# Second mixer: two modulation vectors to TensorE's column groups, GpSimd's low parts of weights to VectorE

## The chip, the cores and the metric

The kernel is one program on one core of a Trainium2 chip. The metric is the device time of the program in microseconds; of the kernel before there are three runs, 2885.76, 2887.93 and 2890.27 us, median 2887.93.

## The reference

Two transformer blocks run one after the other on 256 tokens of width 2048, in float32, batch 1. Each block makes six modulation vectors from a conditioning vector, mixes tokens, and runs a feed-forward part:

```python
mod = silu(c) @ ada_w + ada_b                # 2048 x 12288: six vectors of 2048
sh1, sc1, g1, sh2, sc2, g2 = split(mod, 6)   # numbers 0 to 5
u = rms_norm(h, norm_mix_g) * (1 + sc1) + sh1
h = h + g1 * hybrid_mixer(u, ...)            # u @ w_in, attention of four kinds, @ w_out
u = rms_norm(h, norm_ffn_g) * (1 + sc2) + sh2
h = h + g2 * swiglu(u, ...)
```

The first block has a mixer of two recurrent kinds and a squared-ReLU feed-forward part; the second block, shown above, has a mixer with four kinds of attention (in the code fox, nsa, dil and diff) and ends with one more norm. The change touches the second block's vector 4 (the scale sc2, needed for the feed-forward input) and vector 2 (the gate g1, needed at the mixer's end), and the weights of that mixer.

## The kernel before, in words

All matrices come from HBM once, in pieces ("items") of 128 partitions x 1024 float32, 512 KB, each into one of five buffers named raw (RAW_BUFS, line 26). There are two kinds of items, in one list that is fixed ahead (lines 1908 to 1945): weights of a product, and pieces of a modulation matrix that are strewn between them.

Products run in two float32r parts. For a weight item, ScalarE writes the high part wh from raw, and an engine that is chosen per item writes the low part wl = raw - wh (`prep`, line 274). TensorE then does three matmuls for each weight tile: high x high, high x low and low x high. Four buffers hold pairs of wh and wl. Which engine makes wl is decided by `l_eng` (line 350) from the mark `low` that line 1939 puts on an item: 0 is VectorE; 1 and 2 lead to GpSimd for all or for every second item; 3 compares the two engines' times in a cost model kept in the code (class `_Clock`) and takes GpSimd if it would be done at most 3 us after VectorE. The table LOW (lines 1901 to 1903) sets 3 for the second mixer's input products (qG, kvH, sv, qA, kB, qC, kD, dv0, dv1, qE, kF, fdv) and 2 for most of its output product (pA, 0 to 3). A few places in the code of a stage's turn call `prep(pool)` and fix GpSimd for one item.

A modulation vector comes from 32 items. In one way (`cg` false), VectorE does two accumulating steps for each item, acc = raw x c + acc, on 128 x 512 elements, with one value of the conditioning per partition; the partitions are summed later. In the other way (`cg` true, `ada_cg`, line 320), two items are held until both are there, and TensorE does four matmuls with the conditioning as stationary operand, 32 columns wide, each in its own quarter of TensorE's columns; after four pairs the sum is taken from PSUM by ScalarE (a column vector) or VectorE (a row vector). The first block's vectors 0, 1, 3, 4 and 2 go the second way before; all others go the first way. Two items are then placed in the list at once (line 1942).

The order of every engine's instructions is fixed when the program is built. The builder emits the big matmuls in order, and after each weight tile the function `fill` (line 439) emits other work: steps of evacuations, attention steps (generators), and the next `prep`, by the same cost model. Every instruction emitted updates the model, so a change of one engine's work moves the places of others.

In the trace all engine instructions have the line 169 of a recording helper, so they are told apart by their tiles: raw, wh, wl as above; hTh, hTl and o2h, o2l, oq2h, oq2l the high and low parts of activations; g a PSUM tile of a big product; mx a PSUM tile of small products (three buffers); S score tiles in SBUF; acc sums of modulation vectors; ada the PSUM tile of the second way; csil the conditioning.

Of the kernel before, what the change touches and what calls it, by code (L numbers as in the profile page):

```python
# [178 lines left out]
def two_blocks(ctx, tc, I, out):  # L179
# [47 lines left out]
    items = []  # L227
# [5 lines left out]
    def add_w(pieces, nk, n):  # L233
        items.append({"pieces": pieces, "nk": nk, "n": n})
        return len(items) - 1

    def add_ada(blk, v, q, kp, fin, row, cg):
        items.append({"ada": (blk, v, q, kp), "fin": fin, "row": row, "cg": cg})
# [457 lines left out]
    def col_gen(blk, v, q):  # L696
        a = accs.pop((blk, v, q))
        name = (("mix1", "ffn1"), ("mix2", "ffn2"))[blk][v // 3]
        p = mx()
        if blk == 0:  # L700
            for k in range(4):
                mm(p[:, k:k + 1], a[:, k * 128:(k + 1) * 128], ones[:, 0:1])
        else:
            for k in range(4):
                pe.transpose(p[:, k * 128:(k + 1) * 128], a[:, k * 128:(k + 1) * 128], ident)
            red = small([4], "red")
            junk = wt("junk")
            for k in range(4):
                act.activation(junk[:, k * 128:(k + 1) * 128], p[:, k * 128:(k + 1) * 128], AF.Copy, accum_out=red[:, k:k + 1])
            p = red  # L710
            yield
        b0 = 128 + blk * 64 + (v // 3) * 32 + (v % 3) * 16 + q * 4
        ks = slice(q * 4, q * 4 + 4)
        if v % 3 == 0:
            dve.tensor_add(AB[name][1][:, ks], p[:, 0:4], cols[:, b0:b0 + 4])
        else:
            tmp = small([4], "colt")
            dve.tensor_add(tmp, p[:, 0:4], cols[:, b0:b0 + 4])
            dve.scalar_tensor_tensor(AB[name][0][:, ks], tmp, 1.0, NORM[name][:, ks], op0=ADD, op1=MUL)

    def row_gen(blk, v, q, key, mul):
        while key not in gws:
            yield
        while not slots:
            yield
        slot = k, p = slots.popleft()
        a = accs.pop((blk, v, q))
        t = p.tile([128, UK * 512], FR, name="ah", tag=f"wh{k}")
        h, l = t[:, 0:512], t[:, 512:1024]
        act.activation(h, a, AF.Copy)  # L730
        dve.tensor_tensor(l, a, h, op=SUB)
        yield 3
        if slot[0] < st["n"]:
            slots.append(slot)
        p = mx()
        mm(p, ones_r, h, True, False)
        mm(p, ones_r, l, False, True)
        o = gws[key][:, q * 512:(q + 1) * 512]
        if mul:
            dve.tensor_tensor(o, p, o, op=MUL)  # L740
        else:
            act.activation(o, p, AF.Copy)
        gwn[key] = gwn.get(key, 0) + 1
# [4 lines left out]
    def ada_vecs(blk, vs, key=None, mul=False, cg=False):  # L748
        n = 8 * len(vs)
        for q in range(4):  # L750
            for kp in range(n):
                fin = None
                if kp == n - 1:
                    if key is None:
                        fin = lambda q=q: urgent.extend((clk.wr[clk.key(accs[blk, v, q])][0] + 0.2, col_gen(blk, v, q)) for v in vs)
                    else:
                        fin = lambda q=q: urgent.append((clk.wr[clk.key(accs[blk, vs[0], q])][0] + 0.2, row_gen(blk, vs[0], q, key, mul)))
                ADA.append((blk, vs, q, kp, fin, key is not None, cg))
# [1127 lines left out]
    ada_vecs(1, (0, 1))  # L1886
    ada_vecs(1, (3,))
    n_b = len(ADA)
    ada_vecs(1, (4,))
    ada_vecs(1, (2,), "g1")  # L1890
    n_c = len(ADA)
    ada_vecs(1, (5,), "g2")

    def weight(k):
        if k[0] in ("oB", "pB") or k == "fv" or k[1:] == (0, 0) and k[0] in ("f1", "ga") or k in (("f1", 0, 1), ("f2", 3, 2), ("f2", 3, 3)):
            return 0.0
        if k in ("qG", "kvH", "sv"):
            return 0.5
        return 1.0

    LOW = {k: 1 for k in ("qG", "kvH", "sv", "qA", "kB", "qC", "kD", "dv0", "dv1", "qE", "kF", "fdv")}
    LOW.update({k: 3 for k in LOW if isinstance(k, str)})
    LOW.update({("pA", c): 2 for c in range(4)})
    ai = n_first
    wide = [blocks[n, 0] for n in ("hq", "hf", "hv", "hg", "zq", "zk", "zv", "gg")]
    q_items = [ADA[q * 16:q * 16 + 16] for q in range(4)]
# [21 lines left out]
    for endkey, ntot in phases:  # L1928
        hi = order.index(endkey) + 1
        tot = sum(len(blocks[k].us) * weight(k) for k in order[lo:hi])  # L1930
        tot = tot * 0.5 if endkey[0] == "up" else tot - (3 if endkey[0] == "pA" else 0 if endkey == "fdv" else 24)
        a0, na = ai, ntot - ai
        done = 0.0
        for k in order[lo:hi]:
            b = blocks[k]
            b.idx = []
            for u in b.us:
                b.idx.append(add_w(*u))
                items[-1]["low"] = k in LOW and (LOW[k] if LOW[k] == 3 else len(b.idx) % LOW[k] == 0)
                done += weight(k)  # L1940
                while ai < ntot and (ai - a0) < na * done / tot:
                    for _ in range(1 + ADA[ai][6]):
                        add_ada(*ADA[ai])
                        ai += 1
        lo = hi
# [200 lines left out]
    b = blocks["f2", 3, 3]  # L2146
# [90 lines left out]
    b = blocks["pB", 0]  # L2237
# [63 lines left out]
    b = blocks["dn", 2, 3]  # L2301
# [45 lines left out]
```

## Time and profile before

| | |
|---|---|
| runs, median | 2887.93 us (2885.76 to 2890.27) |
| profiled execution | 2885.77 us, span 2883.8 us, mean granted TensorE clock 0.972 |
| TensorE matmul (PE) | 2713.4 us busy, 94% |
| VectorE (DVE) | 1783.3 us busy, 62% |
| ScalarE (ACT) | 1246.2 us busy, 43% |
| GpSimd (POOL) | 464.1 us busy, 16% |
| moved | 643.93 MB, mean 223 GB/s |

A busy time counts from an instruction's start to its end, so an instruction that is held up while it runs counts as busy for longer. PE durations overlap, since matmuls are pipelined: how long one really takes of the engine is the distance between two starts. A wait is listed by what ended it. The second mixer lies between some 1632 and 2080 us from the span's start.

### The profile page before, as it was taken

Reading aid. Unit: us, or ns where it says so; the run is one execution under the profiler, and the core shown is the slowest. Engines: PE = TensorE matmul, PEld = TensorE weight load, DVE = VectorE, ACT = ScalarE, POOL = GpSimd, SP = SyncE. Lnnn points to the kernel's source line nnn. Section 1 sums busy time; section 2 is a strip of 40 time slices with the busy share of each in tenths; the row PEclk is TensorE's granted clock in tenths of the full one; section 3 lists DMA queues with packets and bytes.
Section 4 is the critical chain, followed back from the end, with each engine's and each line's share of the span. In section 5 each row is a group of like instructions: output and inputs, shape, how many; then the busy total and the mean of one; then the engine's idle time right before and its main releaser. Section 6 shows DMA issues by size and latency. Waiting matters only on the chain.

```text
span 2883.8 us, 44820 instructions
## 1 busy us (share of the span) xinstructions
PE 2713.4 (94%) x17761; PEld 2377.2 (82%) x17761; DVE 1783.3 (62%) x2228; ACT 1246.2 (43%) x1963; POOL 464.1 (16%) x306
## 2 busy tenths in 40 slices
PE   6988999999979999999998899998979999999998
PEld 3666788877869899897997798886769989998997
DVE  1443563655568877778765657677866665554456
ACT  3322354344554444444444436454454443443443
POOL 1000123123040000000002465554520000000001
PEclk8998999999989999999999899999989999999999
DMA  9876775684548888988865675667747777656654
GB/s 337 241 210 194 206 254 181 209 270 147 167 142 295 310 292 296 317 279 296 296 211 168 180 216 166 199 207 239 252 144 233 232 237 236 187 184 193 183 183 146
DMA packets 346594, 643.93 MB, mean 223 GB/s; under 512 B 31488, under 2 KB 50640, under 8 KB 344976
## 3 DMA queue, kind: packets, MB, share of 16 engines
q1 hardware_dynamic: 343296, 628.26, 68.0%
q10 hardware_dynamic: 2336, 10.42, 0.9%
q8 instruction: 139, 2.28, 0.3%
q0 software_dynamic: 752, 2.39, 0.2%
q14 instruction: 71, 0.58, 0.1%
HBM read 636.27 MB, written 4.19 MB: 222 GB/s over the span
## 4 chain that ended last, share of the span: by engine, by line
PE 52%; DVE 7%; DMA 5%; issue 3%; ACT 3%; POOL 2%; SPq 0%; ACTq 0%; POOLq 0%; DVEq 0%
PE g L169 50%; DMA raw<-in_w_ff_dram 3%; PE mx L169 3%; DVE acc L169 2%; DVE wl L169 2%; ACT wh L169 1%; DMA raw<-in_ada_w_dram 1%; POOL wl L169 1%; DVE xres L169 1%; POOL y L169 1%; DMA raw<-in_w_in_dram 0%; DVE S L169 0%; ACT sq L169 0%; DVE y L169 0%; ACT hTh L169 0%
## 5 line engine op out<-in xcount | busy, mean ns | idle before, releaser
L169 DVE TENSOR_TENSOR wl<-raw,wh 128x1024 fp32r<-128x1024 f32 x696 | 871.8, 1258 | 720.6 <-ACT wh L169 713.3
L169 ACT ACTIVATE wh<-raw 128x1024 fp32r<-128x1024 f32 (+2 forms) x817 | 846.5, 1044 | 1078.8 <-PE g L169 683.3
L169 PE MATMUL g<-hTh,wh 128*128 128x256 f32 x3328 | 959.0, 288 | 4.0 <-ACT wh L169 2.3
L169 PE MATMUL g<-hTh,wl 128*128 128x256 f32 x3328 | 945.2, 284 | 1.9 <-POOL wl L169 1.2
L169 PE MATMUL g<-hTl,wh 128*128 128x256 f32 x3328 | 944.0, 284 | 0.3 <-DVE hTl L169 0.3
L169 PEld LDWEIGHTS g<-hTh,wh 128*128 128x128 f32 x3328 | 637.8, 192 | 42.9 <-issue 36.0
L169 PEld LDWEIGHTS g<-hTl,wh 128*128 128x128 f32 x3328 | 640.0, 192 | 1.9 <-DVE hTl L169 0.6
L169 PEld LDWEIGHTS g<-hTh,wl 128*128 128x128 f32 x3328 | 637.4, 192 | 3.0 <-POOL wl L169 1.7
L169 DVE SCALAR_TENSOR_TENSOR acc<-raw,csil,acc 128x512 f32<-128x512 f32 x432 | 391.9, 919 | 64.3 <-DMA raw<-in_ada_w_dram 57.7
L169 PE MATMUL g<-wh,rh 128*128 128x512 f32 x864 | 339.7, 393 | 0.0
L169 PE MATMUL g<-wh,rl 128*128 128x512 f32 x864 | 339.2, 393 | 0.0
L169 PE MATMUL g<-wl,rh 128*128 128x512 f32 x864 | 339.0, 392 | 0.0
L169 POOL TENSOR_TENSOR wl<-raw,wh 128x1024 fp32r<-128x1024 f32 (+3 forms) x121 | 275.8, 2288 | 236.4 <-ACT wh L169 232.3
L169 POOL TENSOR_TENSOR y<-y,gw 128x512 f32<-128x512 f32 x22 | 32.1, 1474 | 1308.1 <-ACT sq L169 749.9
L169 PEld LDWEIGHTS g<-wh,rl 128*128 128x128 f32 x864 | 162.6, 188 | 36.2
L169 PEld LDWEIGHTS g<-wl,rh 128*128 128x128 f32 x864 | 162.7, 188 | 35.7
L169 PEld LDWEIGHTS g<-wh,rh 128*128 128x128 f32 x864 | 162.6, 188 | 35.5
L169 PE MATMUL g<-wh,hTh 128*128 128x512 f32 (+3 forms) x344 | 136.5, 397 | 12.2 <-ACT hTh L169 12.2
L169 PE MATMUL g<-wl,hTh 128*128 128x512 f32 (+3 forms) x344 | 128.4, 373 | 2.5 <-POOL wl L169 2.5
L169 PE MATMUL g<-wh,hTl 128*128 128x512 f32 (+3 forms) x344 | 128.9, 375 | 0.1
L169 PE MATMUL ada<-raw,csil 128*32 128x512 f32 x640 | 107.7, 645 | 16.5 <-DMA raw<-in_w_ada_dram 14.7
L169 PEld LDWEIGHTS g<-wh,hTh 128*128 128x128 f32 x344 | 67.8, 197 | 35.9 <-ACT hTh L169 14.9
(460 smaller groups left out, 2762.5 us busy)
## 6 DMA issues: line engine op xcount, KB each, us to landing
raw<-in_w_ff_dram SPq DMA_DIRECT2D x256, 512.0 KB, 5.3
raw<-in_w_ada_dram SPq DMA_DIRECT2D x192, 512.0 KB, 5.0
raw<-in_ada_w_dram SPq DMA_DIRECT2D x192, 512.0 KB, 5.0
raw<-in_w_in_dram SPq DMA_DIRECT2D x176, 512.0 KB, 5.8
raw<-in_ffn_w_gate_dram SPq DMA_DIRECT2D x88, 512.0 KB, 4.0
raw<-in_ffn_w_up_dram SPq DMA_DIRECT2D x88, 512.0 KB, 3.7
raw<-in_ffn_w_down_dram SPq DMA_DIRECT2D x88, 512.0 KB, 4.1
raw<-in_w_out_dram SPq DMA_DIRECT2D x60, 512.0 KB, 4.6
```

Source lines behind the costliest of these rows:

```text
L169: r = f(out, *a, **kw)
```

## The change

Vectors 4 and 2 of the second block are made in the second way. The table LOW goes, and every item's mark becomes 0, so that VectorE makes all low parts except those that `prep(pool)` fixes.

```diff
     n_b = len(ADA)
-    ada_vecs(1, (4,))
-    ada_vecs(1, (2,), "g1")
+    ada_vecs(1, (4,), cg=True)
+    ada_vecs(1, (2,), "g1", cg=True)
     n_c = len(ADA)
...
-    LOW = {k: 1 for k in ("qG", "kvH", "sv", "qA", "kB", "qC", "kD", "dv0", "dv1", "qE", "kF", "fdv")}
-    LOW.update({k: 3 for k in LOW if isinstance(k, str)})
-    LOW.update({("pA", c): 2 for c in range(4)})
...
-                items[-1]["low"] = k in LOW and (LOW[k] if LOW[k] == 3 else len(b.idx) % LOW[k] == 0)
+                items[-1]["low"] = 0
```

On TensorE, in the product qG of the second mixer (a difference; + is what the change adds):

```order
 L169 MATMUL g<-hTl_13933,wh 128x256
 L169 MATMUL g<-hTh_13929,wl 128x256
+L169 MATMUL ada<-raw,csil 32x512 x4
 L169 MATMUL g<-hTh_13929,wh 128x256
 L169 MATMUL g<-hTl_13933,wh 128x256
```

Groups of four such matmuls stand at 32 more places, between the big matmuls; nothing else is added to TensorE.

On VectorE, ahead of the score tiles of the dil attention (S, with their row maxima dl), before:

```order
L169 TENSOR_TENSOR o2l_14435<-mx,o2h_14434 64x256
L169 SCALAR_TENSOR_TENSOR acc<-raw,csil,acc 128x512 x14
L169 TENSOR_TENSOR colt<-red,cols 128x4
L169 SCALAR_TENSOR_TENSOR Affn_128<-colt,cols 128x4
L169 SCALAR_TENSOR_TENSOR acc<-raw,csil,acc 128x512 x4
L169 SCALAR_TENSOR_TENSOR S_17271<-cb,mx 128x384 x3
L169 TENSOR_REDUCE dl_17272<-S_17271 128x3 x2
```

and in the changed kernel:

```order
L169 TENSOR_TENSOR wl<-raw,wh 128x576
L169 TENSOR_TENSOR colt<-red,cols 128x4
L169 SCALAR_TENSOR_TENSOR Affn_128<-colt,cols 128x4
L169 TENSOR_TENSOR o2l_14441<-mx,o2h_14440 128x256
L169 TENSOR_TENSOR wl<-raw,wh 128x576 x3
L169 TENSOR_TENSOR wl<-raw,wh 128x1024 x4
L169 SCALAR_TENSOR_TENSOR S_17284<-cb,mx 128x384 x3
L169 TENSOR_REDUCE dl_17285<-S_17284 128x3 x2
```

The accumulating steps are gone from VectorE's queue, and low parts that GpSimd made stand there instead.

On GpSimd, at the start of the second mixer (a difference; S and lfp are tiles that it clears, kvH a projection that it copies):

```order
-L169 TENSOR_TENSOR wl<-raw,wh 128x1024 x10
-L169 TENSOR_TENSOR wl<-raw,wh 128x560 x4
-L169 COPY S_14440<-kvH 64x256
-L169 COPY S_14440<-kvH 64x255
-L169 COPY S_14443<-kvH 64x256
-L169 COPY S_14443<-kvH 64x255
-L169 TENSOR_TENSOR wl<-raw,wh 128x560 x4
-L169 TENSOR_TENSOR wl<-raw,wh 128x1024 x32
-L169 TENSOR_TENSOR wl<-raw,wh 128x576 x12
```

Of these the four copies come again in the changed kernel, and none of the low parts. The five `prep(pool)` items of the turn at the mixer's end stay on GpSimd.

## Rows read from the trace of the kernel before

**Rows 1.** The page: span, GpSimd's busy share and TensorE's granted clock in 40 slices

```profile
span 2883.8 us, 44820 instructions
...
POOL 1000123123040000000002465554520000000001
PEclk8998999999989999999999899999989999999999
```

**Rows 2.** Busy time by stage (from:to, length, engines with instruction counts, clock, DMA)

```profile
core 0: us, PE busy (x) PEld busy (x) DVE busy (x) ACT busy (x) POOL busy (x), PEclk, DMA share, GB/s
300.00:700.00 400.00, 390.91 (x2780) 317.37 (x2781) 232.53 (x389) 164.13 (x330) 97.25 (x78) 1.00 0.69 221
1632.00:2080.00 448.00, 412.46 (x2819) 368.63 (x2819) 316.30 (x425) 218.21 (x481) 239.48 (x120) 0.95 0.67 213
2150.00:2800.00 650.00, 650.00 (x4713) 617.26 (x4712) 362.98 (x357) 270.60 (x287) 3.53 (x2) 1.00 0.67 208
1632.00:1640.00 8.00, 5.14 (x23) 4.83 (x23) 6.70 (x13) 5.50 (x8) 2.58 (x1) 0.64 0.95 266
1700.00:1720.00 20.00, 20.00 (x176) 19.66 (x176) 13.04 (x17) 6.26 (x10) 11.65 (x5) 0.74 0.70 212
```

**Rows 3.** TensorE's waits, 1632 to 2080 (total us, times, longest)

```profile
PE mx L169 <- DVE S L169: 16.0, 12, 4.3
...
PE g L169 <- POOL wl L169: 2.7, 4, 1.2
...
PE g L169 <- ACT wh L169: 2.3, 1, 2.3
```

**Rows 4.** VectorE's groups, 1632 to 2080 (busy us, mean ns, idle before)

```profile
L169 DVE SCALAR_TENSOR_TENSOR acc<-raw,csil,acc 128x512 f32<-128x512 f32 x127 | 166.9, 1314 | 54.8 <-DMA raw<-in_ada_w_dram 52.2
L169 DVE TENSOR_TENSOR wl<-raw,wh 128x1024 fp32r<-128x1024 f32 x21 | 35.3, 1679 | 13.6 <-ACT wh L169 11.8 <-PE mx L169 1.8
```

**Rows 5.** The same on VectorE, 2200 to 2500 and 2200 to 2800 (min/median/max ns)

```profile
L169 DVE SCALAR_TENSOR_TENSOR acc<-raw,csil,acc x48: 742/748/754, 2202.7 to 2446.5; 128x512 f32<-128x512 f32 x48
...
L169 DVE TENSOR_TENSOR wl<-raw,wh x212: 1214/1225/1586, 2200.4 to 2797.8; 128x1024 fp32r<-128x1024 f32 x106
```

**Rows 6.** GpSimd's low parts, 1632 to 2080, by shape

```profile
L169 POOL TENSOR_TENSOR wl<-raw,wh 128x1024 fp32r<-128x1024 f32 x76 | 187.1, 2470 | 186.7 <-ACT wh L169 183.4 <-PE mx L169 2.2 <-PE g L169 0.9
L169 POOL TENSOR_TENSOR wl<-raw,wh 128x576 fp32r<-128x576 f32 x16 | 25.2, 1581 | 15.2 <-ACT wh L169 14.6 <-DMA raw<-in_w_in_dram 0.6
L169 POOL TENSOR_TENSOR wl<-raw,wh 128x560 fp32r<-128x560 f32 x8 | 11.9, 1492 | 4.6 <-ACT wh L169 4.4
```

**Rows 7.** Timeline near 1880: VectorE, GpSimd, TensorE (start us, us, [idle before])

```profile
1874.98 11.19 DVE L169 SCALAR_TENSOR_TENSOR acc<-raw,csil,acc 128x512 f32<-128x512 f32 x4 [1.30 <-DMA raw<-in_ada_w_dram]
...
1877.56 5.31 POOL L169 TENSOR_TENSOR wl<-raw,wh 128x1024 fp32r<-128x1024 f32 x2 [0.27 <-ACT wh L169]
...
1886.69 0.54 PE L169 MATMUL mx<-kD,qC 64*128 64x128 f32 x1 [4.32 <-DVE S L169]
```

**Rows 8.** Timeline of TensorE in the first mixer, around one column group

```profile
425.59 0.28 PE L169 MATMUL g<-hTl,wh 128*128 128x256 f32 x1
425.71 0.28 PE L169 MATMUL g<-hTh,wl 128*128 128x256 f32 x1
425.92 1.06 PE L169 MATMUL ada<-raw,csil 128*32 128x512 f32 x8
426.92 0.39 PE L169 MATMUL g<-hTh,wh 128*128 128x256 f32 x1
427.14 0.28 PE L169 MATMUL g<-hTl,wh 128*128 128x256 f32 x1
```

**Rows 9.** Waits of the SP queue and of VectorE, 1632 to 2080

```profile
SPq L169 <- POOL wl L169: 219.2, 85, 9.5
...
DVE acc L169 <- DMA raw<-in_ada_w_dram: 54.2, 19, 14.1
```

**Rows 10.** Column groups, 300 to 700: busy by engine; TensorE's idle before them

```profile
300.00:700.00 400.00, 56.63 (x344) 8.69 (x344) 2.71 (x4) 4.17 (x7) 1.00 0.69 221
...
  DMA raw<-in_w_ada_dram: 7.3, 5
```

## Prediction

> **What bounds the kernel now.** I read the page first. TensorE is busy nearly all of the span; GpSimd has one long busy stretch, slices 25 to 28 of 40, and in the same slices the granted clock dips [rows 1]. That stretch is the second mixer, and it is where the diff acts. Next I cut the program into stages [rows 2]. In the feed-forward stage from 2150 to 2800 TensorE is busy 650.00 of 650.00 us at full clock, with every low part made on VectorE and GpSimd next to idle. In the second mixer, 1632 to 2080, it is busy 412.46 of 448.00 us at a mean granted clock of 0.95. So TensorE is the bound in both; the mixer alone has slack, of two kinds. It idles 448.00 - 412.46 = 35.5 us. And the clock has two levels, so a mean of 0.95 means that 448 x 0.05 = 22.4 us of full-speed work is lost to the lower one. A change here can give back at most 35.5 + 22.4 = 57.9 us.
>
> What does TensorE wait for there? The table of waits [rows 3] has eleven lines: the largest is the score tiles S on VectorE, 16.0 us in 12 waits; low parts from GpSimd end only 2.7 us directly; 2.3 us belong to ScalarE. So VectorE is late, though busy only 316.30 of 448.00 us [rows 2]. Why shows in its own groups. One accumulating step of a modulation vector costs 1314 ns on the mean here, 127 times, and a low part 1679 ns [rows 4]; the same instructions cost 748 ns (742 to 754) and 1225 ns after 2200, where GpSimd does nothing [rows 5]. The difference is GpSimd's subtractions, 76 of 2470 ns, 16 of 1581 and 8 of 1492 [rows 6]. The timeline shows one case [rows 7]: from 1874.98 four accumulating steps last 11.19 us instead of 4 x 0.75 = 3.0, under GpSimd's low parts, and TensorE waits 4.32 us for the score tile queued behind them.
>
> That the two engines exclude each other is what the Trainium skill says too (SBUF — State Buffer, section SBUF: two separate sides): a VectorE instruction with two SBUF inputs and a GpSimd instruction that reads SBUF take one shared port pair in turn, for the whole instruction. The stretched steps agree [rows 4, 5]; by that rule the change frees VectorE wholly, which is the first rival below.
>
> **VectorE and GpSimd, part by part.** The two vectors are 64 items of two steps, 128 steps; 127 begin in this window and go: -166.9 us of VectorE time [rows 4]. The 100 low parts of GpSimd come: 76 x 1.225 = 93.1 us [rows 5]; the 24 narrow ones have no undisturbed row on VectorE, so I scale by GpSimd's ratio, 1.225 x 1581/2470 = 0.78, 18.8 us. The 21 low parts already on VectorE fall from 1679 to 1225 ns, -9.5 us. VectorE ends near 316.3 - 166.9 + 93.1 + 18.8 - 9.5 = 252 us, 56% of the stage: it does not become the bound. GpSimd loses 187.1 + 25.2 + 11.9 = 224 us, none of it on TensorE's path except those 2.7 us. GpSimd keeps the five low parts that the code of the turn at 2080 asks of it by name; I cost that at nothing, since the order of instructions has them where they were. Eight evacuations of the new sums (one on ScalarE or VectorE for each vector quarter) are hidden behind TensorE's stream.
>
> **TensorE pays.** Every pair of items becomes one group of four matmuls, 32 groups. Their price stands in the first mixer, where other vectors already go this way [rows 8]: the matmul before starts at 425.71, 0.12 behind its predecessor, and its successor would come at 425.83; the group starts at 425.92, the next at 426.92 and the one after it only at 427.14, 0.22 behind instead of 0.12. So a group pushes the stream back by 427.14 - 0.12 - 425.83 = 1.19 us, not the 1.06 of its own row. 32 x 1.19 = 38.1 us, all of it on the engine that bounds. Nothing hides it except slack that it fills.
>
> The Trainium skill has a rule against the change here (TensorEngine Tiling (Array Packing), section Tiling Modes, Key Properties): changing the tiling mode drains the engine. The 0.09 us ahead of the group and the 0.10 behind agree; without such a cost the sum would be 32 x 1.00 = 32.0.
>
> **What TensorE gets back.** Of the 35.5 us of idle, 8.00 - 5.14 = 2.9 lie ahead of 1640 [rows 2], most of it ScalarE's 2.3 [rows 3], and stay. Of the other 32.6 I let 6 stay: the score matmuls write three PSUM buffers that VectorE must empty, and it still works 56% of the time, so the 12 waits for S keep about 0.5 us each. That is -26.6 us. Of the 22.4 us of clock, 8 x 0.36 = 2.9 fall before 1640 and 20 x 0.26 = 5.2 between 1700 and 1720, where TensorE is busy 20.00 of 20.00 us with narrow matmuls [rows 2]: these stay. The other 14.3 follow waits and go in their proportion, 26.6/32.6: -11.7 us. Gain 38.3 us, bounded by 0 and by 32.6 + 14.3 = 46.9.
>
> **A wait is added.** A group stands in TensorE's queue and needs both weight items landed; behind it stand all the mixer's matmuls. Before, VectorE took this wait: 54.2 us in 19 waits [rows 9]. In the first mixer, 43 groups in 400 us take 56.63 us of TensorE against 43 x 1.06 = 45.6, so 11.0 us are waits inside groups, and 7.3 us more are shown as waits for the transfer [rows 10]: 0.43 a group. With 32 groups in 448 us, a third less dense, I scale it to 32 x 0.43 x (32/448)/(43/400) = 9 us. The bounds: 0, since the SP queue now waits 219.2 us for GpSimd to free raw buffers [rows 9] and VectorE will free them sooner; and half of VectorE's 54.2, 27 us, since one wait can serve two items. I take 9, by the nearest row.
>
> **Sum.** 38.1 + 9 - 38.3 = +8.8 us. The profiled execution took 2885.77 us for its span of 2883.8, so 2894.6; it stands 2.2 us below the median 2887.93, which carries the sum to 2896.7. I take 2896. Its own range, from waits left at 3 to 12 us and transfers at 5 to 13: 2889 to 2905.
>
> **Rivals.**
> First, faster: the port was the whole trouble. All 32.6 us of waits and the 14.3 us of clock go, and transfers land in time because raw buffers come free sooner: 38.1 - 46.9 = -8.8 us, 2879. For it speak the stretched steps [rows 7] and the stage after 2150 with no idle at all [rows 2]; against it that the scores' three buffers remain, and that the first mixer, with other GpSimd work but the same groups, still idles 400.00 - 390.91 = 9.1 us. It decides where transfers and the waits that are left stay together under 46.9 - 38.1 - 5.8 = 3 us, the 5.8 being what a measurement can tell (below).
>
> Second, slower: the transfers' wait moves to TensorE in full. At 27 us the sum is 38.1 + 27 - 38.3 = +27, 2915. It takes the forecast's place from some 15 us of such waits on. For it: VectorE's wait is real and long, and 64 of these items pass through five raw buffers together with the weights. Against it: the first mixer's 0.43 a group at a DMA share of 0.69, where this stage has 0.67 [rows 2].
>
> Third, a wash: waits go as forecast and transfers cost little, 38.1 + 2 - 40 = 0, 2888.
>
> Fourth, low parts late: 100 of them now stand in VectorE's queue, each behind ScalarE's high part, and the score tiles behind them; if that keeps every wait, 38.1 + 9 = +47, 2935.
>
> **How the numbers follow.** Below 0.2% (5.8 us) a measurement of this kernel cannot tell a difference from none. Forecast 0.48, of it 0.36 slower and 0.12 same; first rival 0.24, of it 0.20 faster and 0.04 same; second 0.12, slower; third 0.12, of it 0.02 faster and 0.10 same; fourth 0.04, slower. That makes faster 0.22, same 0.26, slower 0.52. The range runs from the first rival's 2879 to the second's 2915: half of the first and of the second, and the fourth, lie outside.
>
> **What the profile after would show.** Right: VectorE's low parts at 1.23 us throughout the mixer and its busy time near 250 us; 32 more groups of 1.0 us on TensorE; TensorE's waits for S and for the other VectorE tiles under 10 us; the granted clock of the stage near 0.98; the stage some 9 us longer. Wrong: the stage shorter than 448 us (the gain was under-counted), waits of TensorE for the modulation weights above 15 us (second rival), or waits for low parts or S as long as now (fourth).

## Result, and the profile after

The changed kernel is slower by half a per cent: 2907.55 us median (2902.08 to 2911.49, 8 runs) against 2891.49 (2883.72 to 2900.01, 8 runs) for the kernel before, a ratio of 1.0053 [1.0035, 1.0070]. In the terms of the prediction's sum that is 2887.93 x 0.0053 = 15.3 us, where +8.8 was forecast. The two profiled executions, 2905.57 and 2885.77 us, lie 19.8 us apart, 4 us more than the medians; the one of the kernel before was at the quick end of its runs. The sums below are of these two executions.

The page after, in the rows that answer to [rows 1]: the span, GpSimd's busy tenths and TensorE's granted clock in 40 slices.

```profile
span 2903.7 us, 45170 instructions
...
POOL 1000123122030000000002000000230000000001
PEclk8998999999989999999999998999989999999999
```

GpSimd's long stretch, slices 23 to 29 before [rows 1], is gone, as the change says. In this part of the span the clock dipped in slices 23 and 30 before, at the two ends of the stage; now it dips in 25 and 30, so one dip has moved from the stage's start into its middle.

To compare like with like I cut the stage at the same two pieces of work in both kernels, from the evacuation of the first mixer's last projection to GpSimd's first addition to the residual stream. For the kernel before, the stage by windows (from:to, length, busy time and instructions of PE, PEld, DVE, ACT, POOL, clock, DMA share, GB/s), and then the stretch 1725 to 1790:

```profile
1631.20:2078.80 447.60, 412.06 (x2820) 368.24 (x2820) 315.42 (x426) 218.02 (x482) 238.28 (x120) 0.95 0.67 212
...
1725.00:1790.00 65.00, 61.25 (x499) 56.27 (x498) 54.53 (x90) 40.74 (x118) 32.45 (x14) 1.00 0.57 179
```

The same for the changed kernel:

```profile
1627.30:2098.60 471.30, 446.21 (x3081) 368.25 (x3080) 235.54 (x404) 222.16 (x486) 15.15 (x20) 0.97 0.63 202
...
1725.00:1790.00 65.00, 53.61 (x403) 46.48 (x402) 32.12 (x69) 35.99 (x99) 0.53 (x1) 0.87 0.45 137
```

The stage grew by 471.3 - 447.6 = 23.7 us, and the other stages gave back 4. TensorE's idle time fell from 447.60 - 412.06 = 35.5 us to 471.30 - 446.21 = 25.1, and the full-speed work lost to the lower clock, by the mean, from 22.4 us to 471.3 x 0.03 = 14.1. But take the 65 us from 1725 on. There TensorE idled 3.75 us at full clock before; now it idles 11.4 us, at a mean clock of 0.87, which is another 65 x 0.13 = 8.5 us (a part of it falls into the idle time itself and costs nothing, see the last section). Nearly half of all idle time that the stage has now, and more than half of its lost clock, lie in this one stretch, which was among the best before.

What TensorE waits for in the changed kernel, 1628 to 2098 (total us, times, longest), answers to [rows 3]:

```profile
PE mx L169 <- DVE S L169: 11.6, 4, 6.0
PE ada L169 <- DMA raw<-in_ada_w_dram: 4.8, 9, 1.5
PE g L169 <- ACT wh L169: 3.5, 3, 1.6
PE g L169 <- DVE wl L169: 2.4, 5, 0.8
PE mx L169 <- DVE lfp L169: 2.0, 1, 2.0
...
```

The score tiles S are the largest line still, but its shape is another: 12 waits became 4, and two of these are nearly all of the 11.6 us. TensorE's timeline shows them (start us, us, [idle before, and what ended it]):

```profile
1753.50 0.58 PE L169 MATMUL mx<-ksw,qG 64*128 64x128 f32 x1 [6.05 <-DVE S L169]
...
1766.38 0.58 PE L169 MATMUL mx<-kvH,qG 64*128 64x128 f32 x1 [4.91 <-DVE S L169]
```

Both lie in the stretch 1725 to 1790. Why was VectorE late with S there, when it was busy only 32.12 of 65 us? Its timeline around the first of them:

```profile
1744.19 1.81 DVE L169 TENSOR_REDUCE ns<-S 128x4 f32<-128x512 f32 x2
1750.25 1.23 DVE L169 TENSOR_TENSOR wl<-raw,wh 128x1024 fp32r<-128x1024 f32 x1 [4.24 <-ACT wh L169]
...
1751.76 1.23 DVE L169 TENSOR_TENSOR wl<-raw,wh 128x1024 fp32r<-128x1024 f32 x1
1752.90 1.01 DVE L169 SCALAR_TENSOR_TENSOR S<-cb,mx 128x384 f32<-128x384 f32 x2
```

and ScalarE's in the same microseconds, first and last of eight exponentials, and the high parts behind them:

```profile
1744.91 0.40 ACT L169 ACTIVATE S<-S,ns 128x128 f32<-128x128 f32 x1 [2.83 <-DVE ns L169]
...
1748.68 0.49 ACT L169 ACTIVATE S<-S,ns 128x256 f32<-128x256 f32 x1
...
1749.18 1.99 ACT L169 ACTIVATE wh<-raw 128x1024 fp32r<-128x1024 f32 x2
```

Read it from the end. TensorE waits until 1753.50 for a PSUM buffer. VectorE empties it into S from 1752.90 on, not because it was busy, but because two low parts stand ahead of S in its queue, and the first of them waited 4.24 us, until 1750.25, for ScalarE's high part. ScalarE made that high part only from 1749.18 on, since eight softmax exponentials stood ahead of it. A low part that has nothing to do with the scores joins the two queues, and what was parallel becomes a chain: exponentials, high part, low part, next scores.

The same place in the kernel before. GpSimd, then ScalarE, then VectorE:

```profile
1747.88 2.38 POOL L169 TENSOR_TENSOR wl<-raw,wh 128x1024 fp32r<-128x1024 f32 x1 [7.03 <-ACT wh L169]
```

```profile
1746.76 1.04 ACT L169 ACTIVATE wh<-raw 128x1024 fp32r<-128x1024 f32 x1
```

```profile
1744.95 1.01 DVE L169 SCALAR_TENSOR_TENSOR S<-cb,mx 128x384 f32<-128x384 f32 x2
...
1750.48 1.02 DVE L169 SCALAR_TENSOR_TENSOR S<-cb,mx 128x384 f32<-128x384 f32 x2
```

ScalarE's high part stood behind the exponentials there too. But it was GpSimd that stood still for it, 7.03 us, with nothing of TensorE's behind it, while VectorE went on to S. In sum, VectorE's waits for high parts in the changed kernel, 1628 to 2098, are

```profile
DVE wl L169 <- ACT wh L169: 159.9, 83, 6.6
```

GpSimd had 183.4 + 14.6 + 4.4 = 202 us of such waits before [rows 6], and VectorE 11.8 at its large low parts [rows 4]; so some three quarters of GpSimd's waits now stand in VectorE's queue. Two of the 83, of 4.24 and 6.62 us, stand ahead of the two long waits for S.

The price of a group and the waits for transfers, on TensorE's timeline of the changed kernel:

```profile
1657.31 0.28 PE L169 MATMUL g<-hTh,wl 128*128 128x256 f32 x1
1657.52 1.06 PE L169 MATMUL ada<-raw,csil 128*32 128x512 f32 x8
1658.52 0.39 PE L169 MATMUL g<-hTh,wh 128*128 128x256 f32 x1
1658.74 0.28 PE L169 MATMUL g<-hTl,wh 128*128 128x256 f32 x1
...
1689.23 1.05 PE L169 MATMUL ada<-raw,csil 128*32 128x512 f32 x4 [1.46 <-DMA raw<-in_ada_w_dram]
1690.54 1.05 PE L169 MATMUL ada<-raw,csil 128*32 128x512 f32 x4 [0.25 <-DMA raw<-in_ada_w_dram]
```

The undisturbed group costs 1658.74 - 1657.31 - 2 x 0.12 = 1.19 us, as forecast. The other one came in two halves: the first item's two matmuls ran, and the second item was not there yet. Its halves take 1.05 us each, as long as the whole. So a late second item costs more than its listed wait. Five groups are split like this, with starts 1.31, 1.75, 1.35, 1.28 and 1.84 us apart. Three more of the 31 in this stage ran in two halves too, though no wait is listed for them: they show as one row of about twice the length, 2.16, 2.15 and 2.02 us instead of 1.06. The first of them:

```profile
1784.25 2.16 PE L169 MATMUL ada<-raw,csil 128*32 128x512 f32 x8
```

With the 2.6 us of waits ahead of first halves, transfers cost 7.5 + 3.2 + 2.6 = 13.3 us, where the table of waits lists 4.8.

VectorE's low parts in the changed kernel, 1628 to 2098, answer to [rows 4, 5]:

```profile
L169 DVE TENSOR_TENSOR wl<-raw,wh 128x1024 fp32r<-128x1024 f32 x96 | 116.6, 1224 | 130.9 <-ACT wh L169 130.6
```

They take 1224 ns each, so the stretching by GpSimd is gone. The figure that matters is the other one, 130.9 us of idle time in front of them.

### The profile page after: what moved, and what is told of

The parts are those of the page before. It is cut to its first block, busy times and chain, and to the rows that moved or that the text cites. A ratio compares the mean times of both kernels' runs of the same rounds, so it can differ in the third digit from the quotient of the medians.

```text
span 2903.7 us, 45170 instructions
## 1 busy us (share of the span) xinstructions
PE 2747.6 (95%) x18017; PEld 2375.6 (82%) x18017; DVE 1700.8 (59%) x2207; ACT 1250.0 (43%) x1967; POOL 234.3 (8%) x203
## 5 line engine op out<-in xcount | busy, mean ns | idle before, releaser
L169 DVE TENSOR_TENSOR wl<-raw,wh 128x1024 fp32r<-128x1024 f32 (+2 forms) x799 | 976.4, 1229 | 872.2 <-ACT wh L169 861.7
L169 DVE SCALAR_TENSOR_TENSOR acc<-raw,csil,acc 128x512 f32<-128x512 f32 x308 | 226.4, 751 | 10.7 <-DMA raw<-in_ada_w_dram 6.9
L169 PE MATMUL ada<-raw,csil 128*32 128x512 f32 x896 | 150.1, 640 | 19.8 <-DMA raw<-in_w_ada_dram 13.3
L169 PE MATMUL g<-wh,hTh 128*128 128x512 f32 (+3 forms) x344 | 137.9, 401 | 14.1 <-ACT hTh L169 12.5
L169 POOL TENSOR_TENSOR y<-y,gw 128x512 f32<-128x512 f32 x22 | 32.6, 1501 | 1330.9 <-ACT sq L169 746.7
L169 PEld LDWEIGHTS ada<-raw,csil 128*32 128x32 f32 x896 | 22.2, 110 | 70.9 <-DMA raw<-in_w_ada_dram 31.9
```

The costliest lines, as they stand in the source:

```text
L169: r = f(out, *a, **kw)
```

## Experiments

My theory after the comparison: the forecast was right but for one thing, that low parts in VectorE's queue wait for ScalarE's high parts and hold back S. The rivals: the groups cost more than 1.19 us, or the freed port was worth less than I thought. The first four kernels ran beside the kernel before at 2888.21 us, the other four beside 2888.11.

**One half of the change each.** e1 makes the two vectors on TensorE and leaves the low parts as they were:

```diff
-    ada_vecs(1, (4,))
-    ada_vecs(1, (2,), "g1")
+    ada_vecs(1, (4,), cg=True)
+    ada_vecs(1, (2,), "g1", cg=True)
```

> The two vectors go to TensorE's column groups, the low parts stay as before (GpSimd by the cost model). Theory (a low part on VectorE waits for ScalarE's high part, which stands behind an attention head's exponentials, and the next head's score tiles wait behind it; in the changed kernel that costs 11.4 us of idle and some 8 us of clock between 1725 and 1790): no TensorE wait for S over 2 us in that stretch, and about 10 us less than the changed kernel, so 5 us over the kernel before (ratio 1.000 to 1.003). Rival (the column groups themselves cost the 15 us): within 3 us of the changed kernel, ratio 1.004 to 1.007. VectorE's low parts and sums: GpSimd has no accumulating steps left to collide with, so both expect VectorE's instructions at their undisturbed durations.

Measured: 2888.47 us, ratio 1.0006 [0.9994, 1.0019]. Its stretch 1725 to 1790, and TensorE's waits, 1632 to 2080:

```profile
1725.00:1790.00 65.00, 62.60 (x506) 53.42 (x506) 34.09 (x68) 40.34 (x118) 28.80 (x13) 1.00 0.48 148
```

```profile
PE ada L169 <- DMA raw<-in_ada_w_dram: 3.1, 6, 1.3
PE g L169 <- ACT wh L169: 2.9, 1, 2.9
PE mx L169 <- DVE S L169: 2.8, 7, 0.5
```

The groups pay for themselves, and no more: S falls from 16.0 us [rows 3] to 2.8, with GpSimd at its low parts all the time. So the accumulating steps in VectorE's queue, stretched as they were, held S back. Against my expectation, the low parts that VectorE makes are still stretched, to 1594 ns from 1225 undisturbed [rows 5] (1632 to 2080):

```profile
L169 DVE TENSOR_TENSOR wl<-raw,wh 128x1024 fp32r<-128x1024 f32 x22 | 35.0, 1594 | 86.4 <-ACT wh L169 86.4
```

With the accumulating steps gone, this stretching no longer shows in TensorE's waits.

e2 is the other half: the changed kernel with the two vectors on VectorE again.

```diff
-    ada_vecs(1, (4,), cg=True)
-    ada_vecs(1, (2,), "g1", cg=True)
+    ada_vecs(1, (4,))
+    ada_vecs(1, (2,), "g1")
```

> All low parts go to VectorE, the two vectors stay there as accumulating steps; no column groups are added. Theory (blocked queue): the port is free, so accumulating steps fall from 1314 to about 750 ns and most old waits go, but the two long waits for S in the nsa heads appear here too; about 15 to 20 us under the kernel before (ratio 0.993 to 0.996), long waits for S of 4 us and more between 1725 and 1790. Rival (the groups alone cost time, with their transfers some 50 us, and nothing is blocked): 50 us under the changed kernel, ratio 0.987 to 0.990, no such wait.

Measured: 2894.18 us, ratio 1.0025 [1.0011, 1.0038], slower; I had expected a gain, and that was wrong. VectorE's accumulating steps, and TensorE's two largest waits, 1632 to 2080:

```profile
L169 DVE SCALAR_TENSOR_TENSOR acc<-raw,csil,acc 128x512 f32<-128x512 f32 x127 | 95.1, 749 | 5.0 <-DMA raw<-in_ada_w_dram 2.6
```

```profile
PE mx L169 <- DVE S L169: 21.0, 8, 6.0
PE mx L169 <- DVE o2l L169: 7.6, 2, 5.3
```

The steps fall from 1314 ns [rows 4] to 749, 72 us of VectorE time, and TensorE waits more for S, not less: the longest 6.0 us, as in the changed kernel. The rule on the shared port (the Trainium skill, SBUF — State Buffer, section SBUF: two separate sides) agrees with the 749 ns. It does not say how much of the 72 us lay on TensorE's path, and e2 by itself cannot tell what the free port gained from what the low parts in the queue lost.

**The low parts of two products back to GpSimd.** e3 is the changed kernel, with only the products whose items are made during the stretch from 1725 on (kB and qC) given back:

```diff
-                items[-1]["low"] = 0
+                items[-1]["low"] = 1 if k in ("kB", "qC") else 0
```

> The changed kernel with the low parts of two products, kB and qC (16 items, those prepared while the nsa heads run), fixed on GpSimd. Theory (blocked queue): the waits of 6.05 and 4.91 us for S go with the low clock behind them, 15 to 20 us less than the changed kernel, so level with the kernel before (ratio 0.998 to 1.001). Rival (groups): no more than 3 us less than the changed kernel, ratio 1.004 to 1.007.

Measured: 2890.89 us, ratio 1.0009 [0.9995, 1.0024]. The stretch 1725 to 1790, and the line for S, 1632 to 2080:

```profile
1725.00:1790.00 65.00, 61.81 (x500) 52.96 (x500) 32.21 (x72) 38.35 (x116) 28.36 (x12) 0.99 0.47 147
```

```profile
PE mx L169 <- DVE S L169: 2.7, 6, 0.7
```

Against the changed kernel 0.44% or 13 us come back, a little less than the 15 to 20 expected, with 16 low parts on GpSimd, 12 of them in this stretch. VectorE is as busy as in the changed kernel, 32.21 against 32.12 us, so its load was not the cause: the place in its queue was. TensorE's busy time returns to 61.81 us and the clock to 0.99. This settles the theory for the two long waits, but for the rival that e3's other order did it, which e5 tests. e6 does the same to e2 (vectors on VectorE, kB and qC on GpSimd):

> e2 (accumulating steps on VectorE, all low parts there too) with the 16 low parts of kB and qC on GpSimd. Blocked queue: the long waits for S between 1725 and 1790 go, 12 to 16 us less than e2; GpSimd then collides with accumulating steps in that stretch alone; ratio to the kernel before 0.996 to 0.999, which would beat it. Rival (VectorE is simply too full with both jobs): within 4 us of e2, ratio 1.001 to 1.004.

Measured: 2883.33 us, ratio 0.9986 [0.9973, 0.9999], some 11 us under e2 where 12 to 16 were expected. Its wait for S is 14.4 us in 7, from 21.0: the edit helps here as well. But the long waits between 1725 and 1790 did not all go, as I had expected: one of 3.9 us is left, and e8 shows the cause of such a wait.

**The price of a group.** e4 is the changed kernel with each of the 32 groups issued twice (the second outside the builder's cost model, so that all other instructions keep their order; the sums are scaled by 1/64 for it):

```diff
...
-            for j in range(4):
+            for j in range(8 if blk else 4):
+                last, first = j > 3 or not blk, j < 4
+                j %= 4
...
```

> The changed kernel with each of the 32 new column groups issued twice, one behind the other, from the same raw buffers; the sum is scaled by half. No transfer and no change of mode is added, the rest of every engine's order is the same. If a group's 1.0 us is paid in full on TensorE: 32 us more than the changed kernel (24 to 32 where waits absorb some), ratio to the kernel before 1.013 to 1.017. If TensorE has slack there that groups fill: under 15 us more, ratio under 1.010.

Measured: 2924.73 us (5 runs), ratio 1.0126 [1.0105, 1.0148]. On its timeline:

```profile
1635.87 1.06 PE L169 MATMUL ada<-raw,csil 128*32 128x512 f32 x8
1636.75 1.04 PE L228 MATMUL ada<-raw,csil 128*32 128x512 f32 x8
1637.72 0.39 PE L169 MATMUL g<-hTh,wh 128*128 128x256 f32 x1
```

A second group starts 0.88 us behind the first, so 32 add 28 us; against the changed kernel 0.73%, 21 us, were paid, three quarters. TensorE's idle time in the stage is some 3 us less than in the changed kernel (transfers 2.5 us from 4.8), which takes a part of the rest; where the last 4 us went stays open. The wait for S stays (12.3 us in 4). This lies a little under the 24 to 32 us that I had expected for a full price. So the groups are paid mostly in full, and they are not dearer than forecast.

**Only one vector.** e7 is the kernel before with vector 4 alone on TensorE, 16 groups:

```diff
-    ada_vecs(1, (4,))
+    ada_vecs(1, (4,), cg=True)
```

> The kernel before with only vector 4 on column groups (16 groups), vector 2 and all low parts as before. Price and gain of the groups both halve if they are spread evenly: ratio 0.998 to 1.002. If the collisions of accumulating steps with GpSimd are worst while vector 4 is made (1630 to 1870), the gain is more than half: ratio 0.996 to 0.999. If they are worst for vector 2 (the output product): 1.001 to 1.004.

Measured: 2893.46 us, ratio 1.0012 [1.0000, 1.0025]. It is no better than e1 with both vectors. The 68 accumulating steps that are left between 1632 and 2080 are still stretched, to 1243 ns, and TensorE still waits 14.8 us in 12 for S: half the groups were paid, and nearly all of the earlier wait was kept. The ratio fits two of my three cases; the places decide for the third. The waits for S over 1.5 us stand at 1886.69 [rows 7] and later in the kernel before, and at 1893 and later here, behind the last group of vector 4.

**A rule in place of a table.** If the trouble is VectorE standing still for a high part, then those items alone should go to GpSimd. e5 is the changed kernel, with mark 3 for the second mixer's input products and another rule for it: GpSimd takes the low part if the model has ScalarE's clock more than 3 us ahead of VectorE's.

```diff
-        n = it["nk"] * it["n"]
-        h = clk.t["act"]
-        a = max(h, clk.t["dve"]) + 0.07 + n * 1.042e-3
-        b = max(h, clk.t["pool"]) + 0.1 + n * 2.2e-3
-        return pool if b <= a + 3.0 else dve
+        return pool if clk.t["act"] - clk.t["dve"] > 3.0 else dve
...
-                items[-1]["low"] = 0
+                items[-1]["low"] = 3 if isinstance(k, str) else 0
```

> The changed kernel with a rule for the second mixer's input products: a low part goes to GpSimd only where the builder's model has ScalarE's queue over 3 us ahead of VectorE's, which is 15 items, nearly all while the nsa heads run. Blocked queue: as e3, 14 to 18 us less than the changed kernel, ratio 0.999 to 1.002, no wait of TensorE for S over 2 us. Rival (e3 gained by its other order of the heads, not by the queue): the rule picks other items than e3 and keeps half of the loss, ratio 1.003 to 1.005.

Measured: 2887.02 us, ratio 0.9990 [0.9976, 1.0004]: 0.63%, 18 us, under the changed kernel. The stage and the wait for S, 1632 to 2080:

```profile
1632.00:2080.00 448.00, 435.13 (x3062) 357.48 (x3060) 235.59 (x382) 216.96 (x478) 57.24 (x38) 1.00 0.66 210
```

```profile
PE mx L169 <- DVE S L169: 2.6, 6, 0.6
```

Of the rule's 15 items only seven fall between 1725 and 1790, fewer than I had expected, so at least in part it picks others than e3. The long waits are gone all the same, and the ratio lies in the range of the blocked queue and not in the rival's: what e3 gained was not its own order. TensorE has 448.00 - 435.13 = 12.9 us of idle time left in the stage, so there is little slack left to pay the groups' 38 us from.

e8 is the same rule without the groups, on e2:

> e2 with the rule of e5 (18 items go to GpSimd). Blocked queue: as e6 or a little better, since the rule also catches heads of other kinds: 12 to 18 us less than e2, ratio 0.995 to 0.999. Rival (VectorE too full): within 4 us of e2, ratio 1.001 to 1.004.

Measured: 2874.21 us (6 runs, 2870.34 to 2876.54), ratio 0.9945 [0.9925, 0.9966]. It beats both kernels, and e2 by 0.80% or 23 us, more than expected. VectorE's accumulating steps, 1628 to 2098, and GpSimd's timeline, 1725 to 1790:

```profile
L169 DVE SCALAR_TENSOR_TENSOR acc<-raw,csil,acc 128x512 f32<-128x512 f32 x127 | 102.5, 807 | 7.0 <-DMA raw<-in_ada_w_dram 4.6
```

```profile
1746.73 5.14 POOL L169 TENSOR_TENSOR wl<-raw,wh 128x1024 fp32r<-128x1024 f32 x2 [46.06 <-ACT wh L169]
...
1765.51 10.34 POOL L169 TENSOR_TENSOR wl<-raw,wh 128x1024 fp32r<-128x1024 f32 x4 [6.38 <-ACT wh L169]
```

The rule gives GpSimd 18 low parts (between 1628 and 2080 it makes 19, one of them for the turn at the mixer's end) instead of 100, at the places where by the model VectorE would have stood still. So the accumulating steps cost 807 ns instead of 1314 and TensorE pays for no group. The wait for S, 15.1 us in 8, and a clock of 0.95 remain, near those of the kernel before; against e2, S falls by 5.9 us and the 7.6 us for o2l are gone. Against the kernel before, the accumulating steps give back 166.9 - 102.5 = 64 us of VectorE and the program 0.55%, 16 us. So some of the port's time probably did lie on TensorE's path; no run separates that from the other order of the instructions.

A long wait in the stretch is left here as in e6. VectorE, then TensorE:

```profile
1747.82 4.59 DVE L169 SCALAR_TENSOR_TENSOR acc<-raw,csil,acc 128x512 f32<-128x512 f32 x2
```

```profile
1753.32 0.58 PE L169 MATMUL mx<-kvH,qG 64*128 64x128 f32 x1 [3.98 <-DVE S L169]
```

Two accumulating steps take 4.59 us instead of 1.5, beside GpSimd's two low parts from 1746.73 on, and S stands behind them. So the shared port still costs TensorE 4 us where an accumulating step meets a low part on GpSimd just ahead of S. The Trainium skill (Perfetto Trace Analysis, section Optimizing Scalar/DVE Operations) warns that moving work between GpSimd and VectorE might not help because they share a port; here 18 chosen low parts on GpSimd took 0.8% off e2.

## Why the prediction came out as it did

The direction and the range held, and the time was short by 6.5 us of the sum (15.3 measured, 8.8 forecast). In the profiled pair the stage grew by 23.7 us where some 9 were forecast. Of the signs that were named, the low parts at 1.23 us, VectorE near 250 us, the 32 groups and the clock near 0.98 (0.97) came; TensorE's waits for VectorE's tiles were 11.6 + 2.4 + 2.0 = 16 us, not under 10.

- **The page was misread in one place.** GpSimd's stretch is slices 23 to 29, not 25 to 28, and the clock dips in 23 and 30, not in the slices between [rows 1]. The sums rest on the windows [rows 2] and not on this.
- **TensorE pays: right.** It pays 1.19 us a group [rows 8], on the timeline of the changed kernel and, from the other side, in e4: 38.1 us for 32 groups. One of them starts at 1611.28, ahead of the stage as cut, so the stage holds 36.9.
- **A wait is added: too small, and in another form.** 9 us were forecast and 13.3 found. Most of it, 7.5 + 3.2 us, lies in groups that run as two halves, and only 4.8 us are listed as waits.
- **VectorE part by part: right.** The low parts take 1224 ns (1225 forecast), and VectorE is busy for 236 us (252 forecast).
- **What TensorE gets back: this term was mis-sized.** 38.3 us were forecast: 26.6 of waits and 11.7 of clock. Of waits 35.5 - (25.1 - 4.8) = 15.2 were found. The clock gave 22.4 - (14.1 - 3.3) = 11.6, without the 3.3 us of low clock that fall into the two long waits (last section). The sum by the measured terms is 36.9 + 13.3 - 15.2 - 11.6 = 23.4, against 23.7 for the stage; the clock's two digits alone leave 2 us open. That the clock came out as forecast was luck: it was to go in proportion to the waits, and 15.2 us of waits would have given 14.3 x 15.2/32.6 = 6.7.
- **The failing step** is the one that let "6 stay": "VectorE must empty" the three buffers, "and it still works 56% of the time, so the 12 waits for S keep about 0.5 us each". I sized a wait by VectorE's busy share. What decides is what stands ahead of S in its queue, and that may stand still while VectorE is idle. Outside of 1725 to 1790 the estimate came near: there are 25.1 - 11.4 - 4.8 = 8.9 us of such idle time, and I had let 6 + 2.9 = 8.9 stay (that the two are equal is chance).
- **The sum's own range was added up wrongly at its upper end.** With waits left at 12 us, transfers at 13 and the clock in proportion, it is 38.1 + 13 - 29.6 = +21.5, so 2909 and not 2905.
- **The fourth rival was the mechanism.** "Low parts late: 100 of them now stand in VectorE's queue, each behind ScalarE's high part, and the score tiles behind them." I gave it 0.04 and priced it all or nothing, at +47. It came true in one stretch, for 11 us of idle time and the clock that followed. The evidence stood in my own rows: GpSimd's low parts waited 183.4 us for wh [rows 6]. I took their durations and counted the idle time of an engine off the path as free. It was free only as long as it was GpSimd's.
- **The first rival, the port as the whole trouble, fell with e2**: port free, steps at 749 ns, and a slower kernel. The port is a part of the trouble all the same, as the wait of 3.98 us in e8 shows.

## What to carry to other kernels

When an instruction moves to another engine, its wait moves with it: read the idle time in front of it in the old place, and name what will stand behind it in the new queue. An engine that is busy half of the time can still be late, if its queue holds an instruction that waits for a third engine; give such instructions to an engine on which nothing else hangs. And a stall on a shared port is worth only what the wait behind it on the bounding engine is worth: take the stalled work away (e1) and the port no longer shows in TensorE's waits; leave it ahead of S (e6, e8) and a wait of 4 us stays.

## What the runs showed of the hardware

Each of the two long waits cost twice. After the 6.05 us wait for S, the big matmuls of the changed kernel started 0.21 us apart instead of 0.12 until 1759.9, while the granted clock was 0.50, the lower of its two levels. Two of these matmuls, then windows right behind the two waits:

```profile
1759.09 0.41 PE L169 MATMUL g<-hTh,wh 128*128 128x256 f32 x1
1759.30 0.41 PE L169 MATMUL g<-hTl,wh 128*128 128x256 f32 x1
```

```profile
1753.50:1760.00 6.50, 6.50 (x29) 5.85 (x30) 3.58 (x8) 2.83 (x13) 0.00 (x0) 0.50 0.43 138
...
1766.40:1772.00 5.60, 5.60 (x31) 4.95 (x32) 3.56 (x8) 1.96 (x9) 0.00 (x0) 0.65 0.33 97
```

TensorE is busy throughout both, so the low clock costs 6.5 x 0.50 + 5.6 x 0.35 = 5.2 us there. The other 3.3 of the stretch's 8.5 us fall where TensorE mostly stood still, and cost next to nothing. So the two waits, 11.0 us, brought 5.2 us more. And a group of four matmuls in column groups takes 1.06 us, two of the four alone 1.05, and a second group of four starts 0.88 us behind the first: what is paid is the length of the stream, not the number of columns in use.
